# A two-layer hybrid decoder trunk on one core: the turns of the query groups placed 6.5 units behind their group, their scores where they were, and another machine under the scheduler

## The chip, the core and the metric

The kernel runs on one core of one Trainium2 chip, as a single program. The time is device microseconds of that core for one execution, median of several. Before the change three runs took 1003.49, 1003.59 and 1004.76 us.

A core has five engines with a queue of instructions each: TensorE (PE in the profile; PEld is its loading of the stationary operand), VectorE (DVE), ScalarE (ACT), GpSimd (POOL) and SyncE (SP), which here issues the weight loads. An engine works through its own queue in order, and semaphores make it wait for others.

## The reference, cut to what matters

x is 256 tokens of width 1024, mem 256 more. Two layers, each FFN, mixer, FFN; the first mixer is an mLSTM (layer 0), the second a sliding-window attention (layer 1), and both have four cross-attention heads over mem beside them.

```
def rms_norm(x, g):
    xf = x.astype(jnp.float32)
    y = xf * lax.rsqrt(jnp.mean(xf * xf, axis=-1, keepdims=True) + EPS)
    return (y * g.astype(jnp.float32)).astype(x.dtype)
...
def swiglu(x, w_in, w_out):
    gate, up = jnp.split(x @ w_in, 2, axis=-1)
    return (jax.nn.silu(gate) * up) @ w_out
...
    q = apply_partial_rope(rms_norm(q, q_norm_g), cos, sin) * B_HD ** -0.5
...
        s = jnp.einsum('bqhgd,bkhd->bhgqk', qn, kn)
        s = jnp.where(valid, s, -jnp.inf)
        m = jnp.maximum(jnp.max(s, axis=-1, keepdims=True), sink)
        p = jnp.exp(s - m)
        denom = jnp.sum(p, axis=-1, keepdims=True) + jnp.exp(sink - m)
        return jnp.einsum('bhgqk,bkhd->bqhgd', p / denom, vn)
...
    for i in range(DEPTH):
        x = x + 0.5 * swiglu(rms_norm(x, ffn1_norm_g[i]), ffn1_w_in[i], ffn1_w_out[i])
        hn = rms_norm(x, mix_norm_g[i])
...
        y_mem = memory_heads(xq, mem_k, mem_v, xa_q_norm_g[i], xa_k_norm_g[i])
        x = x + jnp.concatenate([y_tok, y_mem], axis=-1) @ w_out
        x = x + 0.5 * swiglu(rms_norm(x, ffn2_norm_g[i]), ffn2_w_in[i], ffn2_w_out[i])
```

## The kernel before

**Weights.** All products are fp32 to full accuracy: each operand is split into a high and a low part, and a product is three matmuls, high by high, high by low, low by high (L227 to L229, helper mm3). The weights come from HBM in tiles of 128 x 1024 (`wtile`, load issued by SP at L220, buffer wr, five of them). ACT makes the high part of a tile (wh, L213 CAST), DVE the low part (wl, L214), eight buffers each. So the cast of a tile can only be done when PE has finished with the tile eight before it.

**Stages.** They run one after another and PE goes from one to the next without a pause planned: keys and values of mem (0 to 33 us), FFN 1 (to 215), mixer A (to 348), FFN 2 (to 528), FFN 1 of layer 1 (to 708), mixer B (to 819), FFN 2 (to the end).

**Norms.** Between two stages stands a norm (class Norm). For each quarter of the new x, `put` makes its split form times the gain, and squares it (acc, ACT L134, added up on DVE at L282). After the last quarter `fold` adds the two halves of acc (DVE L286), and splits that: ACT casts the high half of `sums` (L247, tile u), DVE subtracts for the low half (L248, tile u). `chain` has PE multiply both halves with a matrix of ones (onesr), two matmuls at L304, and DVE works the root out of their result (L315 and on). The next stage's first weight matmuls don't need the root, only the groups' ends do; the chain is therefore put behind the first 84 or so of them, by LAT's norm=8.5.

**Order.** PE and SP run the program in the order in which Python writes it (`manual_schedule`, for PE and SP only). That order is made by the class Weave: the main program is a generator that yields after a few matmuls, and side chains (norm chains, turns, scores, products) are spawned with a delay. Weave keeps a clock of modelled PE time, in us; a chain whose delay has passed goes ahead of the main program at its next yield. The delays are the entries of LAT. On ACT, DVE and POOL the order is the framework's: its scheduler plays the program on a modelled machine and takes, on each of these engines, what is ready there first.

**Turns and scores.** A group of query columns (256) is produced by 48 weight matmuls with the tokens as rows. For the cross heads `cross_spawn`, for the windowed heads the loop at the end of `mixer_b`, copy the group out and scale it, and spawn `queries`, with the delay LAT's cross or query. `queries` has PE transpose the rows (L238, "turn", four transposes of 128 x 128), ACT empties the result into a tile of queries (L134 with the scale gqk or gcut), and spawns `head` for each of two heads, with the delay cross_s (plus cross_m for the second) or head (plus head_m). `head` issues the scores (cross: L233 with kT; windowed: L962 puts the mask into two banks, L967 adds the products), the maxima on DVE (L971, L972), the exponentials on ACT (L134), and, after further delays, the transposes of the probabilities and the products with the values.

So the distance from a group to its scores is cross + cross_s or query + head; where between the two ends the turn stands is what the two parts say.

**Names that the change and the prediction touch:** LAT (L53 to L55), `queries` and `head`, the cast of sums and its low half (L247, L248 in `split_plain`), L304 in `chain`, L213 and L214 in `split`, the copy of the values of mem to vM (ACT, L456), the store and two loads of gd (gate rows of mixer A, ACT's queue, L753 and L756), and `kernel`, where the TileContext is opened.

Of the kernel before, what the change touches and what calls it, by code (L numbers as in the profile page):

```python
# [32 lines left out]
def constants():  # L33
# [16 lines left out]

LAT = dict(pieces=1, norm=8.5, mnorm=8.0, mrest=6.0, finish=18.0, raw=4.0, x0=2.5, fold=5.0, mkeys=7.2, cross=9.5, cross_s=1.5,  # L53
           cross_m=3.7, cross_p=8.7, cross_o=3.0, gates=20.0, scores=2.2, scores_m=8.4, num=6.9, num_r=7.5,
           keys=5.5, keys_d=7.2, query=9.0, head=1.5, head_m=2.5, head_p=9.3, head_o=4.0)  # L55


WARM = 18
# [40 lines left out]
def tile_trunk(ctx: ExitStack, tc: tile.TileContext, a, out):  # L99
# [305 lines left out]
    def head_norm(dst, src, n, hsc):  # L405

        f = head_factor(src, n, hsc)
        hd = src.shape[2] // n
        tt(out=dst.rearrange("p h (m d) -> p h m d", m=n), in0=src.rearrange("p h (m d) -> p h m d", m=n),
           in1=f.unsqueeze(3).to_broadcast([P, 2, n, hd]),  # L410
           op=ALU.mult)
# [14 lines left out]
    def memory():  # L426
# [22 lines left out]
        def keys(gi, kr):  # L449
            nc.scalar.copy(kT[gi], turn(kr))  # L450
            return
            yield

        def late(raw, gr):
            with tc.issue_after(last[0].ins):
                nc.scalar.copy(raw, gr.ps)  # L456
            return
            yield

        def sums():  # L460
            for c2 in range(4):
                x0.square(xT[c2], c2 == 0)
                yield 1.5
            x0.fold()
            yield LAT['fold']
            yield from x0.chain()

        def finish(raw):
            for c2 in range(4):
                norm.square(memT[c2], c2 == 0)  # L470
                yield 2.0
            norm.fold()
            yield LAT['mnorm']
            yield from norm.chain()
            yield LAT['mrest']
            for h in range(2):
                nc.vector.tensor_scalar(vM[:, h], vM[:, h], norm.rc[:, h:h + 1], None, op0=ALU.mult)
            hsc = head_scales(norm.zc, P, False)
            for i in range(2):
                yield 3.0  # L480
                kr = unit(F32)
                head_norm(kr, raw[i], 2, hsc)
                wv.spawn(keys(i, kr), LAT['mkeys'])

        raw = [unit(F32) for _ in range(2)]
        for gi in range(4):
# [11 lines left out]
            dst = raw[gi] if gi < 2 else vM[:, :, (gi - 2) * 256:(gi - 1) * 256]  # L498
            wv.spawn(late(dst, gr), LAT['raw'])
            if gi == 1:  # L500
                nc.sync.dma_start(con, a["con"])
            if gi == 2:
                for c2 in range(4):
                    nc.sync.dma_start(xT[c2], a["xT"][:, 2 * c2:2 * c2 + 2])
        wv.spawn(sums(), LAT['x0'])
        wv.spawn(finish(raw), LAT['finish'])
# [564 lines left out]
```

## Time and profile before

| what | us |
|---|---|
| median of three runs | 1003.59 |
| the profiled execution's own time | 1004.76 |
| span of the profile | 1003.0 |
| PE busy | 993.9 |
| PE's loads of the stationary operand busy | 975.7 |
| DVE busy | 664.6 |
| ACT busy | 531.9 |
| POOL busy | 29.4 |
| weight casts on ACT (L213), 347 of them | 356.9 |
| low parts on DVE (L214), 347 of them | 414.5 |

The span is that of the instructions, 1.76 us shorter than the execution's own time. In a row of a timeline stand the start, the duration, the engine, the line, the operation, what is written and read (without the buffers' numbers), how many instructions in a row are taken together, and in brackets how long the engine was idle before and what it waited for. PE's matmuls overlap: a duration of 0.28 us goes with a spacing of about 0.11, and it is the spacing that counts. In a row of waits stand the waiting engine, tile and line, what was waited for, the total, how often, and the longest.

### The profile page before, as it was taken

How to read it: one execution, taken by the hardware profiler on the slowest of the kernel's cores; microseconds unless marked ns; L12 is line 12 of the kernel's file. 1: busy time of each engine (PE TensorE's matmuls, PEld its weight loads, DVE VectorE, ACT ScalarE, POOL GpSimd, SP SyncE). 2: the span in 40 equal slices, each digit the busy share in tenths (PEclk: the TensorE clock that was granted, in tenths of full speed). 3: DMA queues.
4: the chain of work that ended last, by engine and by line, in shares of the span. 5: the costliest groups of instructions: out<-in, count | busy, mean ns of one | idle time of the engine just before them, and what ended most of it. 6: DMA issues, size and time to landing. Idle time of an engine off the chain costs nothing.

```text
span 1003.0 us, 20581 instructions
## 1 busy us (share of the span) xinstructions
PE 993.9 (99%) x8560; PEld 975.7 (97%) x8560; DVE 664.6 (66%) x1080; ACT 531.9 (53%) x779; POOL 29.4 (3%) x27
## 2 busy tenths in 40 slices
PE   8999999999999999999999999999999999999998
PEld 6999999999999999999999999999997899999998
DVE  5897665578756686666568666656777767666551
ACT  5765445456666554444445444545577755544440
POOL 1001000000101000000000000000122000000000
PEclk9999999999999999999999999999999999999999
DMA  9777655666634566665666666566641247666550
GB/s 308 256 225 214 192 181 179 199 179 193 188 129 145 169 210 190 193 198 177 190 204 201 197 196 191 171 198 200 195 142 64 89 146 228 193 195 188 184 168 22
DMA packets 173204, 182.70 MB, mean 182 GB/s; under 512 B 7124, under 2 KB 168328, under 8 KB 173112
## 3 DMA queue, kind: packets, MB, share of 16 engines
q1 hardware_dynamic: 171872, 179.60, 57.8%
q8 instruction: 67, 1.10, 0.4%
q10 hardware_dynamic: 1016, 1.58, 0.4%
q0 software_dynamic: 224, 0.22, 0.2%
q14 instruction: 25, 0.20, 0.1%
HBM read 180.32 MB, written 1.05 MB: 181 GB/s over the span
## 4 chain that ended last, share of the span: by engine, by line
PE 93%; ACT 3%; DVE 2%; DMA 1%; issue 0%; SPq 0%; ACTq 0%; DVEq 0%
PE bank L227 30%; PE bank L229 30%; PE bank L228 30%; PE bank L233 2%; ACT u L134 1%; PE bank L238 1%; ACT wh L213 1%; DMA wr<-in_mem_w_kv_dram 1%; DVE wl L214 1%; PE bank L1004 1%; ACT xh L134 0%; DVE col L972 0%; DVE acc L282 0%; PE bank L304 0%; DVE col L971 0%
## 5 line engine op out<-in xcount | busy, mean ns | idle before, releaser
L214 DVE TENSOR_TENSOR wl<-wr,wh 128x1024 fp32r<-128x1024 f32 (+1 forms) x347 | 414.5, 1197 | 268.4 <-ACT wh L213 267.1
L213 ACT CAST wh<-wr 128x1024 fp32r<-128x1024 f32 (+1 forms) x347 | 356.9, 1031 | 385.8 <-PE bank L228 357.6
L227 PE MATMUL bank<-xh,wh 128*128 128x256 f32 x1544 | 428.0, 277 | 0.0
L229 PE MATMUL bank<-xh,wl 128*128 128x256 f32 x1544 | 426.8, 276 | 0.1
L228 PE MATMUL bank<-xl,wh 128*128 128x256 f32 x1544 | 426.7, 276 | 0.0
L229 PEld LDWEIGHTS bank<-xh,wl 128*128 128x128 f32 x1544 | 290.1, 188 | 0.3 <-DVE wl L214 0.3
L227 PEld LDWEIGHTS bank<-xh,wh 128*128 128x128 f32 x1544 | 290.0, 188 | 0.1
L228 PEld LDWEIGHTS bank<-xl,wh 128*128 128x128 f32 x1544 | 289.9, 188 | 0.1
L227 PE MATMUL bank<-u,wh 128*128 128x256 f32 x896 | 249.3, 278 | 0.0
L228 PE MATMUL bank<-u,wh 128*128 128x256 f32 x896 | 247.6, 276 | 0.0
L229 PE MATMUL bank<-u,wl 128*128 128x256 f32 x896 | 247.6, 276 | 0.0
L227 PEld LDWEIGHTS bank<-u,wh 128*128 128x128 f32 x896 | 168.3, 188 | 1.7 <-issue 1.7
L228 PEld LDWEIGHTS bank<-u,wh 128*128 128x128 f32 x896 | 168.3, 188 | 0.1
L229 PEld LDWEIGHTS bank<-u,wl 128*128 128x128 f32 x896 | 168.2, 188 | 0.0
L227 PE MATMUL bank<-wh,xh 128*128 128x256 f32 x208 | 59.6, 287 | 0.5 <-ACT t L997 0.5
L228 PE MATMUL bank<-wl,xh 128*128 128x256 f32 x208 | 57.9, 278 | 0.0
L229 PE MATMUL bank<-wh,xl 128*128 128x256 f32 x208 | 57.8, 278 | 0.0
L516 DVE TENSOR_TENSOR t<-bank,rb 128x256 f32<-128x256 f32 x88 | 36.1, 420 | 6.8 <-PE bank L229 6.8
L227 PEld LDWEIGHTS bank<-wh,xh 128*128 128x128 f32 x208 | 39.1, 188 | 1.2 <-ACT t L997 0.7
L228 PEld LDWEIGHTS bank<-wl,xh 128*128 128x128 f32 x208 | 39.1, 188 | 0.1
L229 PEld LDWEIGHTS bank<-wh,xl 128*128 128x128 f32 x208 | 39.0, 188 | 0.0
L134 ACT ACTIVATE u<-bank,col,col 128x256 f32<-128x256 f32 (+1 forms) x48 | 24.9, 530 | 15.2 <-DVE col L975 7.9
(183 smaller groups left out, 674.1 us busy)
## 6 DMA issues: line engine op xcount, KB each, us to landing
wr<-in_ffn_w_in_dram SPq DMA_DIRECT2D x176, 512.0 KB, 4.5
wr<-in_ffn_w_out_dram SPq DMA_DIRECT2D x80, 512.0 KB, 3.8
wr<-in_a_w_in_dram SPq DMA_DIRECT2D x28, 512.0 KB, 3.8
wr<-in_b_w_in_dram SPq DMA_DIRECT2D x14, 512.0 KB, 4.3
wr<-in_a_w_out_dram SPq DMA_DIRECT2D x12, 512.0 KB, 3.2
wr<-in_b_w_out_dram SPq DMA_DIRECT2D x12, 512.0 KB, 3.2
wr<-in_ffn_w_out_dram SPq DMA_DIRECT2D x16, 256.0 KB, 2.8
wr<-in_mem_w_kv_dram SPq DMA_DIRECT2D x7, 512.0 KB, 8.1
```

What stands on the lines that cost most here:

```text
L134: ins = nc.scalar.activation(*args, **kw)
L213: last[0] = nc.scalar.copy(hi[:, i * n:(i + 1) * n], src[:, i * n:(i + 1) * n])
L214: tt(out=lo[:, i * n:(i + 1) * n], in0=src[:, i * n:(i + 1) * n], in1=hi[:, i * n:(i + 1) * n].bitcast(F32), op=ALU.subtract)
L227: nc.tensor.matmul(ps, wh, xh, start=start, stop=False, skip_group_check=True)
L228: nc.tensor.matmul(ps, wh, xl, start=False, stop=False, skip_group_check=True)
L229: nc.tensor.matmul(ps, wl, xh, start=False, stop=stop, skip_group_check=True)
L233: nc.tensor.matmul(ps, lhsT, rhs, start=start, stop=stop, skip_group_check=True)
L238: nc.tensor.transpose(ps, src, ident[:k, :k])
L516: tt(out=t[:, m], in0=ps[m][:, :T], in1=x.rb, op=ALU.mult)
L1004: nc.tensor.matmul(o[es[e], cs], vr[:, i, js], pTs[e][:, src], start=i == 0, stop=i == 1, skip_group_check=True)
```

## The change

Two edits. In LAT, the turn of a cross group comes 6.5 instead of 9.5 units behind the group and its first scores 4.5 instead of 1.5 units behind the turn; the turn of a windowed group 6.5 instead of 9.0, its scores 4.0 instead of 1.5 behind it. The totals, 11.0 and 10.5, stay. And the TileContext is told to play the program on its other model of the machine (the one built for timing) when it orders the engines ACT, DVE and POOL.

```
-LAT = dict(pieces=1, norm=8.5, mnorm=8.0, mrest=6.0, finish=18.0, raw=4.0, x0=2.5, fold=5.0, mkeys=7.2, cross=9.5, cross_s=1.5,
+LAT = dict(pieces=1, norm=8.5, mnorm=8.0, mrest=6.0, finish=18.0, raw=4.0, x0=2.5, fold=5.0, mkeys=7.2, cross=6.5, cross_s=4.5,
            cross_m=3.7, cross_p=8.7, cross_o=3.0, gates=20.0, scores=2.2, scores_m=8.4, num=6.9, num_r=7.5,
-           keys=5.5, keys_d=7.2, query=9.0, head=1.5, head_m=2.5, head_p=9.3, head_o=4.0)
+           keys=5.5, keys_d=7.2, query=6.5, head=4.0, head_m=2.5, head_p=9.3, head_o=4.0)
...
-    with tile.TileContext(nc) as tc:
+    with tile.TileContext(nc, schedule_with_timeline_sim=True) as tc:
         tile_trunk(tc, aps, out)
```

PE keeps its 8332 rows, with the turns and some scores at other places in the two mixers; SP's order stays. ACT has 689 rows before and after, DVE 1040 and 1038 (rows of equal form that stand together count as one); their order differs in many places, in all stages. Three of them follow, where rows with - are before and rows with + after; the numbers behind the names are those of the buffers in the order of the program.

**The norm at the end of mixer A**, on ACT. acc_4363 holds the folded squares, u_4435 is `sums`; the wh are casts of the first weight tiles of the FFN that follows.

```order
 L213 CAST wh_4722<-wr_4720 128x1024
 L213 CAST wh_4752<-wr_4750 128x1024
+L213 CAST wh_4782<-wr_4780 128x1024
 L247 CAST u_4435<-acc_4363 128x256
-L213 CAST wh_4782<-wr_4780 128x1024
 L213 CAST wh_4812<-wr_4810 128x1024
 L213 CAST wh_4854<-wr_4852 128x1024
```

The cast of the sums now stands behind the weight cast that followed it. The same norm on DVE, with the low parts of the same tiles (wl), the fold (L286) and the low half of the sums (L248); L315 is the first step of the root:

```order
-L214 TENSOR_TENSOR wl_4681<-wr_4678,wh_4680 128x1024
+L214 TENSOR_TENSOR wl_4723<-wr_4720,wh_4722 128x1024
 L286 SCALAR_TENSOR_TENSOR acc_4363<-acc_4363 128x256
-L214 TENSOR_TENSOR wl_4723<-wr_4720,wh_4722 128x1024
-L248 TENSOR_TENSOR u_4435<-acc_4363,u_4435 128x256
 L214 TENSOR_TENSOR wl_4753<-wr_4750,wh_4752 128x1024
 L214 TENSOR_TENSOR wl_4783<-wr_4780,wh_4782 128x1024
+L248 TENSOR_TENSOR u_4435<-acc_4363,u_4435 128x256
 L315 TENSOR_SCALAR t_4551<-bank_4548 128x256
 L317 TENSOR_TENSOR t_4551<-bank_4548,t_4551 128x256
```

The low half has moved behind the low parts of two weight tiles, the later of which belongs to the cast that passed the sums on ACT. The other four norms between stages have the same move on both engines: the cast of the sums behind the one weight cast that followed it, the low half behind that tile's low part.

**The end of the first stage**, on ACT. acc_712 is the square of the first quarter of x, vM the values of mem, the wh the last tiles of the first stage and the first of the FFN.

```order
 L134 ACTIVATE xh_411<-u_108,gcol_99 128x256 x2
 L456 COPY vM_128<-bank_314 128x2x256
+L134 ACTIVATE acc_712<-u_101 128x512
 L213 CAST wh_470<-wr_468 128x1024
 L213 CAST wh_502<-wr_500 128x1024
-L456 COPY vM_128<-bank_380 128x2x256
 L213 CAST wh_536<-wr_534 128x1024
 L213 CAST wh_569<-wr_567 128x1024
 L213 CAST wh_604<-wr_602 128x1024
-L134 ACTIVATE acc_712<-u_101 128x512
+L456 COPY vM_128<-bank_380 128x2x256
 L213 CAST wh_638<-wr_636 128x1024
```

The square has moved ahead of five weight casts, and the second copy of vM behind three.

**The second query group of mixer B**, on ACT, before. bank_9459 is its turn on PE, u_9464 the tile of queries that the scores of its heads read; u_9404 to u_9442 are exponentials of the two heads of the group before it.

```order
L134 ACTIVATE u_9405,col_9388<-bank_9390,col_9387,col_9188 128x128
L134 ACTIVATE u_9405,col_9388<-bank_9390,col_9387,col_9188 128x256
L134 ACTIVATE col_9388<-col_9387 128x4
L134 ACTIVATE u_9441,col_9425<-bank_9426,col_9424,col_9188 128x128
L134 ACTIVATE u_9441,col_9425<-bank_9426,col_9424,col_9188 128x256
L134 ACTIVATE u_9442,col_9425<-bank_9427,col_9424,col_9188 128x128
L134 ACTIVATE u_9442,col_9425<-bank_9427,col_9424,col_9188 128x256
L134 ACTIVATE col_9425<-col_9424 128x4
L247 CAST u_9217<-bank_9454 128x256
L134 ACTIVATE u_9464<-bank_9459,gcut_123 128x512
L247 CAST u_9278<-bank_9484 128x256
```

And after the change, where the turn of the same group is bank_9472, its tile of queries u_9477, and u_9452 and u_9453 are the exponentials of the second head before it:

```order
L134 ACTIVATE col_9376<-col_9375 128x4
L247 CAST u_9224<-bank_9423 128x256
L646 COPY t_9470<-bank_9465 128x512
L134 ACTIVATE col_9436<-col_9435 128x4
L213 CAST wh_10096<-wr_10094 128x1024
L134 ACTIVATE u_9452,col_9436<-bank_9437,col_9435,col_9188 128x128
L134 ACTIVATE u_9452,col_9436<-bank_9437,col_9435,col_9188 128x256
L134 ACTIVATE u_9453,col_9436<-bank_9438,col_9435,col_9188 128x128
L134 ACTIVATE u_9453,col_9436<-bank_9438,col_9435,col_9188 128x256
L134 ACTIVATE u_9477<-bank_9472,gcut_123 128x512
L247 CAST u_9224<-bank_9491 128x256
```

The tile of queries still stands behind the exponentials of the head before it. (L646 copies transposed probabilities of a cross head, the L247 split its product with the values.) On PE twelve weight matmuls, two products L233 and four transposes of probabilities stood between the turn and the first scores that read the tile; now twenty-four weight matmuls, four products and ten transposes of probabilities do.

## The prediction

> **What bounds the kernel now.** I read the page first, then the windows by stage, then what TensorE waits for. On the page, each engine's row gives its busy time, and the chain row divides the chain that ended last by engine.
>
> ```profile
> span 1003.0 us, 20581 instructions
> PE 993.9 (99%) x8560; PEld 975.7 (97%) x8560; DVE 664.6 (66%) x1080; ACT 531.9 (53%) x779; POOL 29.4 (3%) x27
> ...
> PE 93%; ACT 3%; DVE 2%; DMA 1%; issue 0%; SPq 0%; ACTq 0%; DVEq 0%
> ...
> L213 ACT CAST wh<-wr 128x1024 fp32r<-128x1024 f32 (+1 forms) x347 | 356.9, 1031 | 385.8 <-PE bank L228 357.6
> ```
>
> TensorE (PE) is the bound: 993.9 of 1003.0 us. The last row matters as much: ScalarE's (ACT's) weight casts spend 357.6 us waiting until PE has finished with an older tile. A cast that stands in ACT's queue is usually not late; it is closed by PE. The same is not true of what stands behind it.
>
> ```profile
> 348.00:528.00 180.00, 180.00 (x1590) 180.00 (x1590) 118.39 (x159) 90.61 (x111) 0.00 (x0) 1.00 0.62 192
> ...
> 708.00:819.00 111.00, 108.63 (x894) 97.85 (x893) 79.72 (x215) 75.40 (x178) 15.92 (x8) 1.00 0.40 128
> ```
>
> These are windows of an FFN and of the second mixer (start and end, length, then PE busy and its count). In the FFN PE runs 1590 matmuls in 180.00 us without a gap, so one costs 0.113 us. In mixer B 111.00 − 108.63 = 2.4 us are open. PE's waits (total, times, longest) say where:
>
> ```profile
> PE bank L967 <- ACT u L134: 1.4, 1, 1.4
> ...
> PE bank L228 <- DVE wl L214: 0.9, 1, 0.9
> PE bank L227 <- ACT t L997: 0.5, 1, 0.5
> ```
>
> The first and third are in mixer B; that is nearly all that the new distances can win back. Any new gap of PE, on the other hand, is paid in full.
>
> **The change, part by part.** No arithmetic is added or removed: PE has 8332 rows in its order before and after, ACT 689. The weight loads on the queue of SP keep their order. The sum is therefore one of waits.
>
> **1. The five norms between stages: +6.9 us.** ACT casts the folded squares (L247), VectorE (DVE) makes their low half (L248), and PE adds the halves over partitions with two L304 matmuls at a place fixed by LAT's norm=8.5. The order rows show that both now stand behind one more weight tile: the cast of the sums behind one more L213, the low half behind one more L214. Before, around 357 us:
>
> ```profile
> 355.55 0.41 ACT L247 CAST u<-acc 128x256 fp32r<-128x256 f32 x1 [0.33 <-DVE acc L286]
> 356.57 0.42 DVE L248 TENSOR_TENSOR u<-acc,u 128x256 fp32r<-128x256 f32 x1
> 356.68 1.06 ACT L213 CAST wh<-wr 128x1024 fp32r<-128x1024 f32 x1 [0.72 <-PE bank L228]
> 356.91 2.36 DVE L214 TENSOR_TENSOR wl<-wr,wh 128x1024 fp32r<-128x1024 f32 x2
> 357.91 0.39 PE L304 MATMUL bank<-u,onesr 128*128 128x256 f32 x2
> 359.18 0.42 DVE L315 TENSOR_SCALAR t<-bank 128x256 int32<-128x256 int32 x1
> ```
>
> The low half was complete at 356.99; PE's second L304 started one spacing after the first, at 358.02. The margin is 1.03 us. The cast at 356.68 waited 0.72 us for PE, and PE's place there does not change, so it ends at 357.74 as before. Now the L247 follows it (to 358.15), and DVE does both weight tiles first: the second L214 starts 0.03 after its cast, at 357.77, and takes 1.23; the next row on DVE starts some 0.08 before its recorded end (356.91 + 2.36 = 359.27, L315 at 359.18). So L248 runs 358.92 to 359.34, and with 0.05 to reach PE the second L304 is late by 359.39 − 358.02 = 1.37 us. (The 0.03 is that of the cast at 536.42 and its L214 just below, the 0.05 that of an L214 and the L229 behind it, in part 2.) The other four, each with the cast that gets ahead, its L214 and L304:
>
> ```profile
> 223.63 1.05 ACT L213 CAST wh<-wr 128x1024 fp32r<-128x1024 f32 x1 [0.74 <-PE bank L228]
> ...
> 224.71 1.23 DVE L214 TENSOR_TENSOR wl<-wr,wh 128x1024 fp32r<-128x1024 f32 x1 [0.59 <-ACT wh L213]
> ...
> 224.86 0.39 PE L304 MATMUL bank<-u,onesr 128*128 128x256 f32 x2
> ```
> ```profile
> 536.42 1.06 ACT L213 CAST wh<-wr 128x1024 fp32r<-128x1024 f32 x1 [0.83 <-PE bank L228]
> 537.51 1.23 DVE L214 TENSOR_TENSOR wl<-wr,wh 128x1024 fp32r<-128x1024 f32 x1 [0.89 <-ACT wh L213]
> 537.65 0.39 PE L304 MATMUL bank<-u,onesr 128*128 128x256 f32 x2
> ```
> ```profile
> 716.29 1.05 ACT L213 CAST wh<-wr 128x1024 fp32r<-128x1024 f32 x1 [0.84 <-PE bank L229]
> ...
> 717.37 1.23 DVE L214 TENSOR_TENSOR wl<-wr,wh 128x1024 fp32r<-128x1024 f32 x1 [0.89 <-ACT wh L213]
> 717.41 0.40 PE L304 MATMUL bank<-u,onesr 128*128 128x256 f32 x2
> ```
> ```profile
> 827.50 1.06 ACT L213 CAST wh<-wr 128x1024 fp32r<-128x1024 f32 x1 [0.77 <-PE bank L228]
> 827.68 2.35 DVE L214 TENSOR_TENSOR wl<-wr,wh 128x1024 fp32r<-128x1024 f32 x2
> 828.73 0.39 PE L304 MATMUL bank<-u,onesr 128*128 128x256 f32 x2
> ```
>
> The working is the same: start of L214 + 1.23 − 0.08 + 0.42 + 0.05 against first L304 + 0.11. That gives 226.33 − 224.97 = 1.36; 539.13 − 537.76 = 1.37; 718.99 − 717.52 = 1.47; and with the second L214 starting when the cast is done (828.59) 830.21 − 828.84 = 1.37. With 1.37 the sum is **6.94**, say 6.9. All weight casts wait for PE, so each L247 is shut in until PE's own release: this cannot be made up later, since PE has no slack in the FFNs. Queued behind the waiting L304 on PE are the weight matmuls of the next stage, ready but in order. A bound from below: should one of the five find its tile cast early, 1.4 less; should PE get past the wait, nothing.
>
> [...]
>
> **2. The start: +0.5 us.** ACT's square of x (acc, L134) moves ahead of two weight casts, and the copy of vM moves behind three more.
>
> ```profile
> 31.44 2.00 ACT L213 CAST wh<-wr 128x1024 fp32r<-128x1024 f32 x2
> ...
> 32.53 2.36 DVE L214 TENSOR_TENSOR wl<-wr,wh 128x1024 fp32r<-128x1024 f32 x2 [0.24 <-ACT wh L213]
> ```
> ```profile
> 33.81 0.19 PEld L229 LDWEIGHTS bank<-xh,wl 128*128 128x128 f32 x1 [0.32 <-DVE wl L214]
> ```
> ```profile
> L134 ACT ACTIVATE acc<-u x7: 616/618/634, 22.5 to 817.6; 128x512 f32<-128x512 f32 x7
> ```
>
> PE already waits at 33.81 for an L214 that waits for the casts. The first L214 ends at 32.53 + 1.23 = 33.76, 0.05 before. Putting 0.62 us of ACT ahead of them delays it by 0.53 (0.09 overlaps, as above); bounds 0 and 0.6. On DVE a small operation on the sinks moves behind a weight tile; PE waits there for a load that lands late anyway, so 0.
>
> **3. Mixer A: +0.35 us.** Turns of the cross queries come 36 matmuls (36 × 0.113 = 4.1 us) earlier, while the copy that empties them stands on ACT behind the two loads of gd, which wait for its store.
>
> ```profile
> 247.68 0.52 ACTq L753 DMA_DIRECT2D gd_dram<-u  x1
> ...
> 248.57 1.03 ACT L213 CAST wh<-wr 128x1024 fp32r<-128x1024 f32 x1
> ...
> 249.34 0.86 ACTq L756 DMA_DIRECT2D u<-gd_dram  x2
> ...
> 250.24 0.59 ACT L610 COPY u<-bank 128x512 f32<-128x512 f32 x1 [0.63 <-issue]
> ```
>
> The store now also stands behind the cast of 248.57, which ends at 249.60. With the 1.66 us from store to loads and the 0.86 of the loads' issue, less what the cast no longer takes behind them, the copy runs at about 252.1 to 252.7; PE, counted matmul by matmul through its new order, wants it at about 252.5. With 0.15 at a later product I take 0.35 in all, from 0 to 1.0 (one cast uncovered).
>
> **4. Mixer B: −1.4 us.** The wait that may go:
>
> ```profile
> 746.49 0.93 PE L967 MATMUL bank<-u,u 64*128 64x128 f32 x8
> ...
> 750.02 0.46 ACT L134 ACTIVATE u<-bank,col,col 128x128 f32<-128x128 f32 x1 [1.34 <-DVE col L975]
> ...
> 754.39 0.73 ACT L134 ACTIVATE u<-bank,gcut 128x512 f32<-128x512 f32 x1
> ...
> 755.17 0.93 PE L967 MATMUL bank<-u,u 64*128 64x128 f32 x8 [1.45 <-ACT u L134]
> ...
> 756.03 0.38 PE L227 MATMUL bank<-wh,xh 128*128 128x256 f32 x1
> ```
>
> The scores at 755.17 wait 1.45 us for the evacuation of their own queries (754.39), which stood on ACT behind the exponentials of two heads, 750.02 to 754.3, about 2.0 a head. After the change one group of twelve weight matmuls (1.4) and further products and transposes stand between that turn and these scores: from the end of the scores before, I count about 7.0 us of PE work. The evacuation needs, from the same point, 2.6 for the maxima (scores ended at 747.42, their exponentials began at 750.02), 2.0 for one head's exponentials and 0.73 for itself, in all 5.4. So this wait goes with 1.6 to spare: −1.45. The others stay or are replaced by some of their size. Bounds: −2.4 (all open time goes) and +1.45 (a new wait as long as the old).
>
> **Sum:** 6.9 + 0.5 + 0.35 − 1.4 = +6.4 us. The profiled execution took 1004.76 (span 1003.0 plus 1.76 around it), so it would take 1011.2 and the span 1009.4. It was the slowest of the three shown; against their median 1003.59 the same sum gives **1010.0**.
>
> **Rivals.**
> - **The norms stay covered** (not slower). Mechanism: L304 is late only if its cast is released less than about 1.4 us earlier than now; with PE's release that much earlier, term 1 is 0 and the sum is −0.55, 1003.0; with all of mixer B's 2.4 won, 1002.0, and below 1001.6 only if the start's wait goes too. For it: the program is the same up to the norms, and DVE is only 66% busy. Against: all five gates (0.72 to 0.84 us) end with PE's own position. 0.08, of which 0.03 faster.
> - **PE passes the wait.** Term 1 near 0: again 1003.0. Against: at 755.17 PE ran nothing, though L227 had its operands. 0.04.
> - **Mixer B gains a wait**: the evacuations now share ACT with copies and a weight cast (1.05). If one is later than the 1.6 to spare, the old 1.45 is replaced by another: 6.9 + 0.5 + 0.35 + 1.45 = +9.2, 1012.8. 0.12.
> - **The order isn't what decides** (the hardware's waits come from elsewhere, the time is as before): 1003.6. 0.04.
>
> **How the numbers follow.** Forecast 0.72, the rivals 0.28 together. Its own range: 4.5 (mixer B all won, mixer A and start nothing) to 8.5 (nothing won, 0.6 and 1.0 lost) makes 1008.1 to 1012.1. One norm covered takes 1.4 off the lower end, and 0.2 more for the spread of the runs: 1006.5. The third rival with mixer A at 1.0 (+9.85) makes 1013.5 above. About 0.2% (2 us) is what a measurement of this kernel tells from no change. Faster: 0.03. Same: 0.13, from the rest of the first, the second and the fourth. Slower: 0.84.
>
> **What would show it.** Five PE waits on DVE's L248 at L304, 1.3 to 1.5 us each, would bear out term 1; L304 starting right after a weight matmul would refute it. PE's wait near 33.8 should grow to about 0.8. The 1.4 of L967 on ACT should be gone from the waits, and mixer B's window should have about 1 us open apart from its norm. If the span grows by less than 4 us with five such waits, something that I did not see was won back; if it grows without them, the mixers did it.

## The result and the profile after

The changed kernel takes 1015.40 us in the median of four executions (1013.56 to 1016.5), the kernel before 1004.17 beside it; the ratio is 1.0109 with the interval [1.0089, 1.0128]. It is slower by 11.2 us, where 6.4 were forecast and 1013.5 was the upper end of the range. Two of the four executions, 1016.05 and 1016.5, have a mean granted clock of 0.998; the other two, 1.0, took 1013.56 and 1014.75.

The profiled execution took 1016.05, its span is 1014.2. The page of the kernel after, its engine rows:

```profile
span 1014.2 us, 20588 instructions
PE 997.9 (98%) x8560; PEld 978.3 (96%) x8560; DVE 666.6 (66%) x1080; ACT 531.1 (52%) x779; POOL 25.5 (3%) x27
```

PE does the same 8560 matmuls and is busy 4 us longer, which is a first hint that some of them ran slower; the other 7 us are gaps. PE's waits after the change (what waited, for what, total, times, longest):

```profile
PE bank L304 <- DVE u L248: 4.5, 5, 0.9
PE bank L227 <- ACT wh L213: 1.6, 1, 1.6
...
PE bank L238 <- ACT u L610: 1.2, 1, 1.2
PE bank L1004 <- ACT u L134: 1.0, 1, 1.0
...
PE bank L962 <- ACT t L646: 0.7, 1, 0.7
```

The scores' 1.4 us on L967 are gone, as forecast. The five of L304 are there, as forecast; they are listed with 0.9 each, since the 0.39 us of the first matmul of a pair count as busy, and by the starts of the two matmuls each pair is 1.18 longer. Not forecast are L227 with 1.6 us (at the start, 0.4 before), L1004 with 1.0 and L962 with 0.7 (mixer B), and the size of L238 with 1.2 (mixer A, where 0.35 was forecast). The norm at the end of mixer A, in the timeline after:

```profile
361.54 1.06 ACT L213 CAST wh<-wr 128x1024 fp32r<-128x1024 f32 x1 [1.46 <-issue]
...
362.50 0.40 ACT L247 CAST u<-acc 128x256 fp32r<-128x256 f32 x1
...
362.95 0.38 PE L304 MATMUL bank<-u,onesr 128*128 128x256 f32 x1
...
363.77 0.42 DVE L248 TENSOR_TENSOR u<-acc,u 128x256 fp32r<-128x256 f32 x1
...
364.24 0.39 PE L304 MATMUL bank<-u,onesr 128*128 128x256 f32 x1 [0.91 <-DVE u L248]
```

It reads as the prediction worked it out: weight cast, cast of the sums, two low parts, and only then L248, whose end (364.19) lets PE go 0.05 later. The pair is 1.29 us apart instead of 0.11. The first of the pair also waits: the cast of the sums ends at 362.90. The other pairs:

```profile
226.95 0.38 PE L304 MATMUL bank<-u,onesr 128*128 128x256 f32 x1
...
228.24 0.19 PEld L304 LDWEIGHTS bank<-u,onesr 128*128 128x128 f32 x1 [1.10 <-DVE u L248]
228.25 0.39 PE L304 MATMUL bank<-u,onesr 128*128 128x256 f32 x1 [0.91 <-DVE u L248]
```
```profile
544.18 0.38 PE L304 MATMUL bank<-u,onesr 128*128 128x256 f32 x1
...
545.47 0.39 PE L304 MATMUL bank<-u,onesr 128*128 128x256 f32 x1 [0.91 <-DVE u L248]
```
```profile
725.52 0.38 PE L304 MATMUL bank<-u,onesr 128*128 128x256 f32 x1
...
726.82 0.39 PE L304 MATMUL bank<-u,onesr 128*128 128x256 f32 x1 [0.91 <-DVE u L248]
```
```profile
838.65 0.38 PE L304 MATMUL bank<-u,onesr 128*128 128x256 f32 x1
...
839.94 0.39 PE L304 MATMUL bank<-u,onesr 128*128 128x256 f32 x1 [0.91 <-DVE u L248]
```

These rows against those of before are a ruler for the whole run, since both kernels do the same matmuls between two norms. The lag behind before is 2.09 us at the first pair's first matmul (226.95 − 224.86), 5.04 at the second, 6.53, 8.11 and 9.92; each pair itself adds 1.18. The first L304 of all, in the norm of mem, tells the start from the FFN behind it; the kernel before first, then the kernel after:

```profile
53.47 0.28 PE L304 MATMUL bank<-u,onesr 128*128 128x256 f32 x1
```
```profile
55.38 0.28 PE L304 MATMUL bank<-u,onesr 128*128 128x256 f32 x1
```

| stretch | added us | forecast |
|---|---|---|
| start, to the norm of mem | 1.9 | 0.5 |
| the five pairs, 5 x 1.18 | 5.9 | |
| close around the pairs: 0.18 ahead of the first; 0.30 in mixer A (as in sched_only) and 0.30 and 0.40 in two FFNs; 0.25 in mixer B (113.13 us against 111.70 in all_mended, less 1.18); 0.1 behind the last | 1.5 | 6.9 with the row above |
| mixer A, 1.77 without its 0.30 | 1.5 | 0.35 |
| mixer B, 0.63 without its 0.25 | 0.4 | −1.4 |
| sum (the spans differ by 11.2) | 11.2 | 6.4 |

So the norms came out nearly as worked (7.4), and the other three terms were all too kind. What happened in each:

```profile
12.01 0.38 PE L227 MATMUL bank<-wh,u 128*128 128x256 f32 x1 [1.56 <-ACT wh L213]
...
13.27 0.38 PE L228 MATMUL bank<-wl,u 128*128 128x256 f32 x1 [0.88 <-DVE wl L214]
```
```profile
10.00:12.00 2.00, 0.45 (x4) 0.25 (x3) 0.25 (x2) 1.09 (x2) 0.00 (x0) 1.00 1.08 389
...
14.00:17.00 3.00, 3.00 (x19) 3.00 (x18) 2.53 (x4) 1.05 (x1) 0.00 (x0) 0.60 1.09 390
```
```profile
35.72 0.19 PEld L229 LDWEIGHTS bank<-xh,wl 128*128 128x128 f32 x1 [0.83 <-DVE wl L214]
```

The kernel before, in the same stretch:

```profile
13.39 0.39 PE L228 MATMUL bank<-wl,u 128*128 128x256 f32 x1 [0.88 <-DVE wl L214]
```
```profile
14.00:17.00 3.00, 3.00 (x28) 3.00 (x27) 2.69 (x4) 1.72 (x4) 0.00 (x0) 1.00 1.08 389
```

The **start** (the rows with a colon are windows: start and end, length, PE busy and count, then PEld, DVE, ACT, POOL, granted clock, DMA share and GB/s). PE is busy 0.45 of the 2 us ahead of 12, and from 14 to 17 us its clock is 0.60, with 19 matmuls begun where the kernel before has 28. The first L227 is not late (12.01 against 12.13): the late load sets it in both (the cast ahead of it waits for the load until 10.91, and until 11.03 before). The lost time is in the matmuls behind it: from the first L228 to the L229 that waits next, PE takes 22.45 us (13.27 to 35.72) instead of 20.42 (13.39 to 33.81), and only 0.5 of these 2.0 are the longer wait.

```profile
252.10 0.52 ACTq L753 DMA_DIRECT2D gd_dram<-u  x1
...
255.56 0.83 ACTq L756 DMA_DIRECT2D u<-gd_dram  x2
256.44 0.58 ACT L610 COPY u<-bank 128x512 f32<-128x512 f32 x1 [3.26 <-DMA gd_dram<-u]
...
257.08 0.66 PE L238 MATMUL bank<-con,u 128*128 128x128 f32 x4 [1.17 <-ACT u L610]
```

**Mixer A**: from the store of gd to the loads behind it 3.46 us pass, 1.66 before. But for one small exponential and the rest of a weight cast ACT does nothing in that time, and the copy that PE's turn needs is behind the loads. The store goes out as soon as DVE's L749 has made gd's rows; on DVE, before and after:

```profile
246.52 0.41 DVE L748 TENSOR_TENSOR u<-u,u 4x256 f32<-4x256 f32 x1
246.97 0.68 DVE L749 TENSOR_TENSOR_SCAN u<-u,u 4x256 f32<-4x256 f32 x1
```
```profile
249.92 0.41 DVE L748 TENSOR_TENSOR u<-u,u 4x256 f32<-4x256 f32 x1
250.26 1.21 DVE L214 TENSOR_TENSOR wl<-wr,wh 128x1024 fp32r<-128x1024 f32 x1
251.40 0.67 DVE L749 TENSOR_TENSOR_SCAN u<-u,u 4x256 f32<-4x256 f32 x1
```

The new order has put a low part of a weight tile between the two.

### The profile page after: what moved, and what is told of

It reads as the page before. It is cut to its first block, busy times and chain, and to the rows that moved or that the text cites. A ratio compares the mean times of both kernels' runs of the same rounds, so it can differ in the third digit from the quotient of the medians.

```text
span 1014.2 us, 20588 instructions
## 1 busy us (share of the span) xinstructions
PE 997.9 (98%) x8560; PEld 978.3 (96%) x8560; DVE 666.6 (66%) x1080; ACT 531.1 (52%) x779; POOL 25.5 (3%) x27
## 4 chain that ended last, share of the span: by engine, by line
PE 92%; ACT 3%; DVE 2%; DMA 1%; issue 1%; SPq 0%; ACTq 0%; DVEq 0%
PE bank L227 29%; PE bank L229 29%; PE bank L228 29%; PE bank L233 2%; ACT u L134 1%; PE bank L238 1%; DVE wl L214 1%; ACT wh L213 1%; DMA wr<-in_mem_w_kv_dram 1%; PE bank L1004 0%; DMA gd_dram<-u 0%; ACT xh L134 0%; DVE u L248 0%; PE bank L967 0%; PE bank L304 0%
## 5 line engine op out<-in xcount | busy, mean ns | idle before, releaser
L227 PE MATMUL bank<-xh,wh 128*128 128x256 f32 x1544 | 428.2, 277 | 0.0
L229 PE MATMUL bank<-xh,wl 128*128 128x256 f32 x1544 | 426.9, 276 | 0.6 <-DVE wl L214 0.6
L228 PE MATMUL bank<-xl,wh 128*128 128x256 f32 x1544 | 426.8, 276 | 0.0
L229 PEld LDWEIGHTS bank<-xh,wl 128*128 128x128 f32 x1544 | 290.0, 188 | 0.8 <-DVE wl L214 0.8
L227 PEld LDWEIGHTS bank<-xh,wh 128*128 128x128 f32 x1544 | 290.1, 188 | 0.1
L228 PEld LDWEIGHTS bank<-xl,wh 128*128 128x128 f32 x1544 | 289.9, 188 | 0.1
L227 PE MATMUL bank<-u,wh 128*128 128x256 f32 x896 | 249.0, 278 | 0.0
L228 PE MATMUL bank<-u,wh 128*128 128x256 f32 x896 | 247.7, 276 | 0.0
L229 PE MATMUL bank<-u,wl 128*128 128x256 f32 x896 | 247.7, 276 | 0.0
L227 PEld LDWEIGHTS bank<-u,wh 128*128 128x128 f32 x896 | 168.2, 188 | 1.4 <-issue 1.4
L229 PEld LDWEIGHTS bank<-u,wl 128*128 128x128 f32 x896 | 168.4, 188 | 0.0
L228 PEld LDWEIGHTS bank<-u,wh 128*128 128x128 f32 x896 | 168.3, 188 | 0.1
L227 PE MATMUL bank<-wh,xh 128*128 128x256 f32 x208 | 59.7, 287 | 0.0
L228 PE MATMUL bank<-wl,xh 128*128 128x256 f32 x208 | 57.9, 278 | 0.0
L229 PE MATMUL bank<-wh,xl 128*128 128x256 f32 x208 | 57.9, 278 | 0.0
L227 PEld LDWEIGHTS bank<-wh,xh 128*128 128x128 f32 x208 | 39.1, 188 | 0.8 <-issue 0.7
L228 PEld LDWEIGHTS bank<-wl,xh 128*128 128x128 f32 x208 | 39.1, 188 | 0.1
L229 PEld LDWEIGHTS bank<-wh,xl 128*128 128x128 f32 x208 | 39.0, 188 | 0.0
L519 DVE TENSOR_TENSOR t<-t,bank 128x256 f32<-128x256 f32 x88 | 32.6, 413 | 0.0
```

Source lines behind the costliest of these rows:

```text
L227: nc.tensor.matmul(ps, wh, xh, start=start, stop=False, skip_group_check=True)
L228: nc.tensor.matmul(ps, wh, xl, start=False, stop=False, skip_group_check=True)
L229: nc.tensor.matmul(ps, wl, xh, start=False, stop=stop, skip_group_check=True)
L519: tt(out=t[:, m], in0=t[:, m], in1=ps[m][:, T:], op=ALU.mult)
```

## The experiments

Each kernel was timed beside the kernel before.

**lat_only** undoes the scheduler's part.

```
-    with tile.TileContext(nc, schedule_with_timeline_sim=True) as tc:
+    with tile.TileContext(nc) as tc:
```

> The four numbers of LAT changed, the scheduler left on its first model. Theory A (the scheduler's new model makes the loss: the five norms, the start, and, together with the earlier turns, the store of gd in mixer A): the five L304 pairs start 0.11 us apart as before, the start is as before, and the turn of mixer A, 4.1 us earlier on PE, still finds its rows copied since the store of gd keeps its old place. What is left is mixer B, between -1.5 and +1 us: 1002.5 to 1005 beside 1004.2. Theory B (the new distances make the loss): 1010 or more. A wait of PE on L610 at the first turn of mixer A of about 1.3 us would speak for B there.

Measured: 1005.77 us, ratio 1.0015 [1.0006, 1.0024]. The pairs are 0.11 us apart, the start is that of before, mixer A takes 133.05 us from pair to pair in both. Mixer B takes 112.50 instead of 111.32. Its waits:

```profile
PE bank L1004 <- ACT t L997: 0.7, 1, 0.7
PE bank L1004 <- DVE u L248: 0.7, 1, 0.7
PE bank L1004 <- ACT u L134: 0.6, 1, 0.6
```

The loss of 11 us is not in the distances, but they don't win either: the wait of L967 went, and the products L1004 wait 2.0 us in its place. Not all of the 1.2 us that mixer B is longer are waits; point 4 below has the rest.

**sched_only** undoes LAT's part (before, with the scheduler's new model).

> The scheduler's new model alone, LAT as before. Theory A: five waits of L304 on DVE's L248, 1.2 us between the two matmuls of each pair more than before and 0.1 to 0.3 ahead of them, 6.5 to 7 us in all; the start 0.5 to 2 us longer; mixer A without its wait of 1.3 us on L610, as the turn comes 4.1 us later: 1011 to 1014 in all, about 1 to 3 us less than with both edits. Theory B: within 2 us of before.

Measured: 1016.57 us, 1.0128 [1.0093, 1.0163], six executions from 1012.89 to 1025.3, the profiled one 1013.11. All five pairs are 1.29 us apart, mixer A has no wait on L610 (134.53 us, of which the norm is 1.48), and mixer B has its old L967 wait. Theory A holds: the losses at the start and at the norms belong to the scheduler, and mixer A's wait needs both edits. The granted clock is 0.62 from 14 to 17 us here too. The spread was not expected; it comes up again below.

**pin_norms** holds the eleventh (in mixer A and two norms' low parts the tenth) weight tile behind the sums.

```
+    def behind(e):
+        for p in pins:
+            p[e][0] -= 1
+            if p[e][0] == 0:
+                return tc.issue_after(p[e][1].ins)
+        return ExitStack()
...
-            last[0] = nc.scalar.copy(hi[:, i * n:(i + 1) * n], src[:, i * n:(i + 1) * n])
...
+            with behind(0):
+                last[0] = nc.scalar.copy(hi[:, i * n:(i + 1) * n], src[:, i * n:(i + 1) * n])
```

> Both edits, but at the five norms one weight cast on ACT and one low part on DVE are held behind the cast and the low half of the sums (by an order on the same engine, no wait). If the five waits are what I take them for, each L304 pair is 0.11 us apart again and the time falls by 6 to 7 us, to about 1008.5 to 1009.5. If PE would have waited for something else there, by less than 3 us.

Measured: 1012.55 us, 1.0077 [1.0065, 1.0089], 2.9 us less than the changed kernel, not 6 to 7. Yet all five pairs are 0.11 us apart, so the five waits are what they were taken for. The rest is given back at one place, which the waits and the windows show:

```profile
PE bank L248 <- ACT u L622: 3.3, 1, 3.3
```
```profile
251.23:254.64 3.41, 0.95 (x9) 0.74 (x7) 1.43 (x2) 0.94 (x2) 0.00 (x0) 1.00 0.67 164
254.64:261.47 6.83, 5.99 (x28) 5.99 (x29) 2.92 (x5) 3.68 (x6) 2.03 (x2) 0.50 0.48 151
```

(L248 and L622 are L238 and L610 of the changed kernel, ten and twelve lines on.) PE comes 3.6 us earlier to the first turn of mixer A, but the loads of gd go out only 1.6 us earlier (253.97), so PE waits 3.3 us there instead of 1.2, and then its clock is 0.50 for 6.8 us: mixer A takes 139.45 us, 6.4 more than before.

**norm_later** moves the pairs instead.

```
-LAT = dict(pieces=1, norm=8.5, mnorm=8.0, ...
+LAT = dict(pieces=1, norm=10.0, mnorm=8.0, ...
```

> Both edits, and LAT's norm 10.0 in place of 8.5: PE comes to L304 1.5 us later in its order, everything else as it is. The low half of the sums was 1.2 to 1.4 us late, so each pair should be 0.11 us apart and the time fall by 6 to 7 us, as with the held casts, unless the root, 1.5 us later, is then late for the groups' ends: a wait of PE for a bank, and no gain.

Measured: 1019.63 us, 1.0133 [1.0105, 1.0161], but one of the six executions took 1009.82. The pairs are 0.11 us apart here too, the roots are in time, and mixer A gives back the same as in pin_norms (139.47 us). The one of 1009.82, with a clock of 1.0, is near the fall of 6 to 7 us that was expected; the others have 0.996 to 0.998. What is new is in the third FFN of the profiled execution:

```profile
580.00:620.00 40.00, 40.00 (x342) 40.00 (x341) 25.08 (x34) 18.89 (x22) 0.00 (x0) 1.00 0.62 189
```

342 matmuls in 40.00 us is 0.117 us for each, with no wait and a granted clock of 1.00; the FFN of before has 0.113. Over that FFN's 1586 matmuls it makes 7.1 us (186.90 against 179.76). An expectation that looked at waits alone missed it.

**sinks_later** is the kernel before with one small operation moved.

```
-        nc.vector.tensor_scalar(nsink, sink, -1.0, None, op0=ALU.mult)
+        with tc.issue_after(last[1].ins):
+            nc.vector.tensor_scalar(nsink, sink, -1.0, None, op0=ALU.mult)
```

(last[1] is the last low part of a weight tile on DVE.)

> The kernel before, with one thing of the change alone: on DVE the small operation on the sinks (L196), which waited 4.7 us for its load at the head of the queue, stands behind a later weight tile; nothing else moves. My theory of the start: PE does its first matmuls earlier, then waits for the same late load, 1.5 us instead of 0.4 at the first L227, so its pause between 10 and 13.4 us grows, and in some executions its granted clock falls to about 0.6 for 3 us behind that pause, which costs 1.5 us. So the first L227 starts within 0.2 us of before, and the time is 1.5 us longer in the executions with the lower clock (more of them than before) and equal in the others: 1004 to 1005.8. The prediction's step (no cost at all): equal to before in every execution.

Measured: 1005.33 us, 1.0005 [0.9996, 1.0013]. The interval says little; the clock says more: 7 of its 11 executions have 0.998, with 1005.15 to 1007.05 us, against 5 of the 23 of before. The profiled one is of the seven:

```profile
14.00:17.00 3.00, 3.00 (x16) 3.00 (x15) 2.42 (x3) 1.06 (x1) 0.00 (x0) 0.50 1.09 391
```

So the step that I had at nothing lowers the clock in more executions.

**pause_filled** is the changed kernel with work for PE in that pause.

```
+                    for _ in range(7):
+                        dummy()
+                    fill.extend([dummy] * 4)
```

(dummy is one matmul on the zeros of the warm-up; the four stand behind the first L227.)

> Both edits, and eleven matmuls on zeros (to the bank of the warm-up) in PE's pause at the start, seven ahead of the first L227 and four behind it. If the lower clock at 14 to 17 us comes from the pause, the granted clock there is 1.0 in every execution, the first L227 is not later, and the profiled start is 1.5 us shorter: 1013 to 1014.2 in all. If the lower clock has another cause, it stays in half of the executions.

Measured: 1014.83 us, 1.0113 [1.0088, 1.0139]; the clock is 0.999 or 1.0 in all six executions, four of which took 1013.02 to 1015.12 and two over 1020.

```profile
10.00:12.00 2.00, 2.00 (x14) 1.13 (x12) 0.89 (x2) 1.50 (x3) 0.00 (x0) 1.00 1.08 392
...
14.00:17.00 3.00, 3.00 (x28) 3.00 (x27) 2.74 (x4) 1.91 (x3) 0.00 (x0) 1.00 1.08 387
```

With PE busy through the pause, 28 matmuls begin from 14 to 17 us again, and the L229 that waits for the casts starts at 34.36 instead of 35.73. The pause was the cause, and it costs 1.4 us. The second matmul of the first L304 pair of all comes at 53.41 instead of 55.50, another 0.7 earlier, which is not the pause: from 36 to 53 us 153 matmuls begin here, and 146 in the profile of the changed kernel (147 in that of before), all at a clock of 1.00. The last section comes back to that. The two long executions were not profiled; their clock is full.

**gate_loads_later** moves the two loads of gd behind the copies.

```
-        for i in range(2):
-            nc.scalar.dma_start(gb[i], gd[2 * i:2 * i + 2, :].partition_broadcast(P))
...
+        with tc.issue_after(copied[0].ins):
+            for i in range(2):
+                nc.scalar.dma_start(gb[i], gd[2 * i:2 * i + 2, :].partition_broadcast(P))
```

> Both edits, but the two loads of gd in mixer A stand on ACT behind the two copies of the cross queries (L610) that PE's turns wait for. My theory: the wait of 1.2 us of L238 on L610 comes from the loads' wait for the store of gd to land (3.5 us). It should go, nothing else: mixer A 1.3 us shorter, and with the norms' waits still there 1012 to 1014. If the turn waits for the copy for another reason, the wait of about 1.2 us stays.

Measured: 1014.90 us, 1.0112 [1.0088, 1.0136], the profiled execution 1013.62. The wait of L238 on L610 is gone, and mixer A takes 134.60 us instead of 136.00: 1.4 of the 1.5 are this wait. What is left over before, 1.55, is the norm (1.48 in sched_only).

**pause_filled_before** fills the pause of the kernel before (one matmul on zeros ahead of the first L227, four behind it).

> The kernel before, with five matmuls on zeros in PE's pause at the start (one ahead of the first L227, four behind it). The kernel before shows two groups of times, about 1003.8 and 1005.4, the longer ones with a mean clock of 0.998. If those are executions in which the pause lowered the clock, the longer group goes: all near 1003.5 to 1004, median 0 to 0.5 us lower. If not, both groups stay.

Measured: 1003.80 us, 0.9994 [0.9985, 1.0003]; 11 executions from 1003.31 to 1004.81, none with 0.998, where the kernel before beside it has 5 of 23 with 0.998 and 6 of 23 over 1005.6. So the longer group goes with the lowered clock, and none of it is left with the pause filled, which eleven executions make likely and not certain. No execution of that group was profiled: where the clock falls in it is not shown.

**all_mended** puts the holds of pin_norms, the later loads of gd and the filled pause together, and holds the square back:

```
-                act(self.acc, xn, AF.Square)
+                with tc.issue_after(last[0].ins) if self.gi == G_MEM else ExitStack():
+                    act(self.acc, xn, AF.Square)
```

> Both edits, and on top of them every step that I hold for a loss is mended: the sums' cast and low half held ahead of one weight tile at the five norms, the loads of gd behind the cross queries' copies, PE's pause at the start filled with matmuls on zeros, and the square of mem's first quarter held behind the weight casts that it had overtaken. If the list is complete, what is left is the loss in mixer B: the time of lat_only within 1 us, 1004.5 to 1006, mixer A 133.0 to 133.2 us from norm to norm, no granted clock under 0.95 behind 14 us. If something of the new order is missing from the list, 1008 or more.

Measured: 1004.36 us (1004.13 to 1004.62 in 11 executions), 1.0001 [0.9993, 1.001]. All of the 11 us is gone, to within the 1 us of the interval, and mixer A is back at 133.05 us. The waits of mixer B:

```profile
PE bank L1030 <- ACT u L134: 1.0, 1, 1.0
PE bank L988 <- ACT t L671: 0.7, 1, 0.7
```

They are L1004 and L962 of the changed kernel, and they are left. So the list is complete to within that 1 us: no other part of the new order costs more. The square was held back only here, together with the rest.

**cross_only** and **query_only** split the distances (cross=6.5, cross_s=4.5 alone, and query=6.5, head=4.0 alone, on the kernel before).

> The kernel before with cross=6.5 and cross_s=4.5 alone. With all four numbers mixer B took 112.5 us from norm to norm against 111.3, and the largest wait of before (scores L967 on their queries, 1.45 us) was gone, with new waits of the products L1004 in its place. If those come from the windowed heads' turns, this kernel has the time of before, with the 1.45 us wait still there: 1003.5 to 1004.5. If they come from the cross heads', 1005 or more.

> The kernel before with query=6.5 and head=4.0 alone: the other half of the same question. If the windowed heads' turns make both the gain and the new waits, mixer B takes 112.3 to 112.7 us, the wait of L967 is gone and waits of L1004 of about 2 us in sum are there: 1004.5 to 1006. If the new waits come from the cross heads', the gain of 1.45 us is left alone: 1002.3 to 1003.

Measured: cross_only 1004.32 us, 0.9998 [0.9989, 1.0007], mixer B 110.46 us, with the wait of L967 still there (1.3 us); query_only 1003.62 us, 0.9996 [0.9987, 1.0005], mixer B 110.86, without it, and with waits of L1004:

```profile
PE bank L1004 <- ACT u L134: 1.1, 2, 0.9
```

For cross_only the first case that was named came true in the time and in the wait; that mixer B would be 0.9 us shorter was not expected. For query_only neither case did: the new waits are there, but only 1.1 us of them. Each half makes mixer B 0.5 to 0.9 us shorter, and both together (lat_only) make it 1.2 longer. In time neither can be told from before.

**query_7_5** was a try at a better distance (query=7.5, head=3.0, with the pause filled).

> A try to beat both: the kernel before with its pause at the start filled, and the windowed heads' turns 1.5 us earlier only (query=7.5, head=3.0), as much as the scores waited. If the scores' wait goes without the new waits of the products: mixer B 109.9 to 110.5 us, 1002 to 1002.7. If the products' waits come with any earlier turn: 1004 to 1005.

Measured: 1005.09 us, 1.0012 [1.0003, 1.0021], mixer B 112.43. The waits only changed place: a transposition of probabilities (L238, here L241) now waits 1.3 us for its exponentials on ACT.

**cross_filled** joins cross_only and the filled pause.

> The cross heads' turns 3.0 units earlier (cross=6.5, cross_s=4.5), the windowed heads' as before, the scheduler on its first model, and five matmuls on zeros in PE's pause at the start. cross_only alone took 1003.0 us in its executions with full clock and 1004.6 in the others. If the two gains add, all executions lie at 1002.8 to 1003.4: 0.5 to 1 us under the kernel before, and under the changed kernel by 12. If the gain of mixer B was chance, mixer B takes 111.3 us and the time is that of before with its pause filled, 1003.8.

Measured: 1003.67 us, 0.9991 [0.9981, 1.0001]. Six executions took 1002.94 to 1003.67, but five, among them the profiled one, 1004.39 to 1006.25 with a clock of 0.998. The start is not to blame this time; the windows of that execution in mixer B are:

```profile
754.00:756.00 2.00, 0.49 (x3) 0.17 (x4) 1.03 (x5) 2.00 (x10) 0.00 (x0) 1.00 0.32 80
756.00:759.00 3.00, 3.00 (x16) 2.06 (x16) 2.79 (x11) 1.35 (x5) 0.00 (x0) 0.50 0.33 127
```

The wait of the scores for their queries, 1.3 us, lowers the clock behind it in this execution, and mixer B takes 112.05 us instead of 110.46. No version beats the kernel before by more than can be measured; this comes nearest.

## Why the prediction was right and wrong, point by point

**What bounds the kernel** held: the gaps of PE were paid in full (each pair adds 1.18 us of lag), and filling or removing them gave the time back (all_mended, ratio 1.0001). But gaps were not all: the clock and the spacing of the matmuls moved too, and no term of the prediction was about them.

**1. The norms** held in mechanism, place and size: 6.9 forecast, 7.4 found, in all five, and gone in pin_norms, norm_later and all_mended. The split between the two matmuls of a pair was a little off, as the first comes later too, by up to 0.3. The rival that PE passes the wait fell: PE began no matmul in the 1.29 us between the two of a pair (226.95 and 228.25 in the first) while weight matmuls stood ready behind L304. Not even the load of the waiting matmul came ahead of the wait's end (228.24, with the matmul at 228.25).

**2. The start** has two parts. The square on ACT was right: the weight load of the L229 is idle for 0.83 us where it was 0.32, so 0.5 (the square is that of mem, not of x as the prediction and the part on the change say, and it passed five weight casts, not the prediction's two; its place in the order is as shown). The step that failed is the other: "a small operation on the sinks moves behind a weight tile; PE waits there for a load that lands late anyway, so 0". The first half is true. But PE now had its earlier matmuls done sooner and stood still for longer ahead of that load, and the clock fell, to 0.60 from 14 to 17 us. That is 1.5 us in this execution (22.45 − 20.42 − 0.5), of which the first weight tile, 0.1 earlier, gives some back: 1.4 net, as 1.9 − 0.5 leaves. It comes in half of the four; sinks_later has it alone, and pause_filled takes it away. The prediction read the granted clock nowhere, though the page gives it.

The lowered clock is 0.50; the 0.60 here and the 0.62 in sched_only, from 14 to 17 us, are of windows that are only partly under it. It lasts 3.41 us at the start (14.62 to 18.03) and 6.83 in mixer A of pin_norms, and two of the changed kernel's four executions have the mean clock of 0.998 that goes with it. PE was not idle ahead of it: it was busy for 1.74 of the 3.41 us before. The last section has the other runs.

**3. Mixer A**: the mechanism was named (the copies on ACT stand behind the loads of gd, which wait for the store), and the term was mis-sized: 1.5 instead of 0.35. The step that failed is "with the 1.66 us from store to loads": the store took 3.46 us to let the loads go. It also went out 1.1 us later relative to PE (252.10 − 247.68, less the 3.3 us that PE was behind), and not for the reason given: not the weight cast on ACT held it, but DVE's L749, behind a low part of a weight tile that now stands ahead of it. The upper end, 1.0, came from the cast alone. lat_only and sched_only show that the wait needs both edits: the turn 4.1 us earlier, and the new order of the store's chain. Why the store was slow is open. Weight loads fit: the DMA share was 0.53 to 0.78 in each us from 252 to 256, and 0.80, 0.66 and 0.00 in the three from 247 in the kernel before. They were not moved by themselves.

**4. Mixer B**: the wait named is gone, as worked out. The step that failed is "the others stay or are replaced by some of their size". Waits of the products L1004 came, 1.0 us here and 2.0 in lat_only. PE's open time from the second matmul of the pair in mixer B to the next pair, and a stretch without waits ahead of that pair, before and after:

```profile
717.52:828.73 111.21, 108.84 (x896) 98.06 (x894) 81.50 (x219) 77.72 (x182) 15.92 (x8) 1.00 0.37 118
806.00:826.00 20.00, 20.00 (x177) 19.65 (x177) 14.20 (x23) 12.72 (x20) 0.00 (x0) 1.00 0.43 129
```
```profile
726.82:838.65 111.83, 109.79 (x893) 98.77 (x894) 80.53 (x218) 77.40 (x181) 12.20 (x8) 1.00 0.37 117
816.00:836.00 20.00, 20.00 (x172) 20.00 (x171) 15.16 (x22) 12.42 (x19) 0.00 (x0) 1.00 0.47 146
```

The open time fell by 0.3 us only (2.37 to 2.04), where 1.4 were forecast. At the longest new wait a weight cast stands on ACT between the exponentials of two heads (785.39); that the cast makes the wait is likely, and no run moves it. And a part that no term of the prediction has: ahead of the next pair PE begins 172 matmuls in 20 us instead of 177, busy all the time and at full clock. Over the 215 matmuls from 813 us on that is about 0.7 us. The slower spacing (0.118 us, 0.113 before) stands there in all nine profiles in which the windowed turns were moved, and in none of the six others, so it comes with the change; why is open. The two make the +0.4 that took the place of −1.4, still inside the bounds that the prediction had. The split runs show that this cannot be added up from its halves: without the 0.7, which is in query_only and lat_only but not in cross_only, mixer B is 0.9 shorter with the cross turns moved, 1.2 with the windowed ones, and 0.5 longer with both.

One sign that the prediction named is not there: mixer B was to have about 1 us open apart from its norm, and it has 2.04.

**The sum.** Of the 4.8 us that were missing, the start makes 1.4, the norms 0.5, mixer A 1.15 and mixer B 1.8. All four err to the same side. The executions of 1013.56 and 1014.75 have a full clock, so the start's 1.4 should not be in them.

## What to carry to other kernels

When an engine is the bound and its work is in a fixed order, a reordering on the engines that feed it can only be priced at the places where it waits in order: look for what stands one place further back behind an operation that is itself closed by the bound engine. A wait that goes is not free either: ask where the bound engine then stands still, for how long, and whether its clock survives that (0.50 behind a wait of 1.3 us in cross_filled). And a gain at one place is lost again if the next arrival, here a DMA's round trip, doesn't come earlier with it (3.6 us against 1.6 in pin_norms, and PE waited 3.3).

## What the runs showed of the hardware that was not expected

Behind a wait of PE of 1.3 us (cross_filled, mixer B) or 1.56 us (the first L227 of the changed kernel, with 0.88 more at the L228 behind it) the clock is lowered to 0.50 in the profiled execution; cross_only has the wait of 1.3 us too, and its clock is 1.00 from 756 to 759 us. In the traces the lowered clock begins and ends in steps of 3.41 us: it lasts one step in the changed kernel (14.62 to 18.03) and two in pin_norms (254.64 to 261.47), and the two steps of norm_later in the table are 245.76 us apart, which is 72 of 3.413. It goes with PE's busy time in the step ahead; these are the lowest of the fifteen profiles (the end of each kernel left out):

| run | step from (us) | PE busy in its 3.41 us | clock in the next step |
|---|---|---|---|
| norm_later, mixer A | 255.50 | 0.74 | 0.50 |
| pin_norms, mixer A | 251.23 | 0.95 | 0.50 |
| gate_loads_later, start | 10.85 | 1.40 | 0.50 |
| norm_later, start | 9.74 | 1.41 | 0.50 |
| sched_only, start | 9.44 | 1.48 | 0.50 |
| sinks_later, start | 10.41 | 1.55 | 0.50 |
| cross_filled, mixer B | 752.60 | 1.71 | 0.50 |
| the changed kernel, start | 11.21 | 1.74 | 0.50 |
| query_7_5, mixer B | 757.37 | 1.87 | 1.00 |
| pin_norms, start | 8.88 | 1.94 | 1.00 |
| pause_filled_before, mixer B | 751.71 | 1.96 | 1.00 |

So in these traces the line lies between 1.74 and 1.87 us, about half of the step. Of the steps with a lowered clock, one with 2.57 us busy was followed by another (pin_norms, from 254.64), one with 2.88 by the full clock (sched_only, from 12.85). The steps may also be why the same pause counts in some executions only: pin_norms has the long pause of the changed kernel at its start (1.5 us at the first L227, here L237, where that has 1.6), but the pause falls on two steps, counted back from 251.23 (71 steps), and the clock stays at 1.00. The kernel before, with five matmuls on zeros, has no execution at 0.998 in eleven.

The spacing of PE's weight matmuls has two values at a granted clock of 1.00: 0.113 and about 0.118 us. The profiles of before and after have both: the first from 60 to 100 us, say (355 matmuls in each), the second from the first stage to the norm of mem (147 and 146 matmuls from 36 to 53 us, 153 in pause_filled), so that it cancels between them. In mixer B it comes with the moved turns (point 4). In the profile of norm_later a whole FFN ran at it, from one L304 pair to the next, 7.1 us longer. Executions 5 to 12 us above the shortest of the same kernel, with a mean clock of 0.998 or more, occur in sched_only, pause_filled and gate_loads_later too, but not in the kernel before or in all_mended; they were not profiled, so that they are this is likely and not shown. What sets the second spacing off stays open.
